# 32-row diagonal blocks inverted by substitution in a DeltaNet layer, in place of 16-row blocks and two merge products, and another order for the last two head groups

## The chip, the cores and the metric

The kernel runs on one core of a Trainium2 chip. The time is the device time in microseconds of one execution; the kernel before was run three times (median 3007.27 us). One further execution was taken with the hardware profiler; its span runs from the first to the last instruction. A core has the engines TensorE (PE, with its weight loads listed as PEld), VectorE (DVE), ScalarE (ACT), GpSimd (POOL) and SyncE (SP, which here issues the transfers).

## The reference: what is computed

A trunk of two layers works on 272 tokens (16 meta tokens and 256 others) of 2048 features in float32: a gated DeltaNet layer, then a differential-attention layer, each followed by a squared-ReLU MLP. The change lies in the DeltaNet layer alone. It has 32 value heads of 128 features on 16 query and key heads. What matters of it, cut:

```python
def step(S, xs):
    qc, kc, vc, bc, gc = xs
    G = jnp.cumsum(gc, axis=-1)
    decay = jnp.exp(jnp.where(tri_incl, G[..., :, None] - G[..., None, :], -jnp.inf))
    kb = kc * bc[..., None]
    a_kk = jnp.where(tri_strict, jnp.einsum('bhik,bhjk->bhij', kb, kc) * decay, 0.0)
    rhs = jnp.concatenate([vc * bc[..., None], kb * jnp.exp(G)[..., None]], axis=-1)
    sol = lax.linalg.triangular_solve(a_kk, rhs, left_side=True, lower=True, unit_diagonal=True)
    ...
```

For each head and each chunk of tokens a system with a unit lower triangular matrix is solved, and the state S is carried on from chunk to chunk.

## The kernel before, in words

**Order of the work.** The kernel goes through eight groups (line 1075) of four value heads each. A group has four stages of projections on TensorE: keys and queries (`keys`, line 653, four weight tiles), values (`values`, line 803, four), gates (`gates`, line 836, four) and the output product (`gate_out`, line 1048, four), the last one for the group two earlier (`LAG`). A weight tile is 1 MB; SyncE loads it (line 121), ScalarE and VectorE split it into a high and a low part (lines 138 and 140), and TensorE makes three products of each 128-row step of it (`mm3`, lines 153, 156 and 157). Such a step is called a k-step here; a weight tile has 16, a stage 64. There are three buffers for weight tiles and three each for the split halves.

**The planner.** Beside the projections runs the triangular part, written as generators. `Flow` (line 51) holds them with due times: each k-step advances its clock by 3 x 272 / 2400 = 0.34 us (line 158), and a generator's `yield t` puts its next piece t later. `until` (line 83) runs pieces early when the next stage needs them: a third value tile of a group waits until the core of the group before has finished two chunks (lines 809 and 828). This gives the order in which instructions are written; a scheduler then gives each engine its queue, in which an instruction can be pulled ahead while a more urgent one is not ready. Each engine then works its queue strictly in order.

**The triangular part of a group.** The tokens form chunks of 128, 128 and 16 (`CH`). `products` (line 683) makes the matrices `UA` for each chunk and head and writes their 16 x 16 diagonal blocks to memory (`scr`, line 762; the meta-sized last chunk's four blocks to `scr3`, line 744). `solve` (line 779) reads them back with one block a partition (`na`, 64 + 4 partitions), inverts them by substitution on VectorE (`forward`, line 641: 15 steps of a multiply and a reduction, on 16 columns at once, each multiply over 16 x (i + 1) elements), writes the result to memory (lines 793, 794) and loads it into the diagonal blocks of `DT` and `DT3` (lines 797, 801). It is written 40 us of the planner ahead of the core (`SOLVE`; 35 for the last group).

**The core** (line 846) first builds from the 16-row inverses those of 32-row blocks, `merge` (line 881), for chunks 0 and 1: it masks `UA` to the 32-row diagonal blocks, less the 16-row ones (line 884, GpSimd), transposes `DT` in blocks of 32 (line 890, VectorE), makes two products for each of four heads with a copy between them (lines 894, 896, 900), adds (line 902), transposes again (line 904), and makes a third product, `ps_n` (line 908), whose result `NT` serves to solve across the four 32-row blocks by a short series (`apply`, line 962; three products `ps_a`). Then come `ps_w`, the state `ps_s`, the output `ps_o`, and, for chunk 2, products with `DT3` (line 947). The turned outputs (`turned`, line 854, `ps_ot`) are multiplied with the gates, split (`halves`, line 1036) and go into `gate_out`. Small products are float32; the profile lists two records for each.

**The end.** For the last group `HOLD` puts the output product of two groups earlier ahead of the gates (lines 1082 to 1089), and the output products of the last two groups follow.

Of the kernel before, what the change touches and what calls it, by code (L numbers as in the profile page):

```python
# [10 lines left out]
F32 = mybir.dt.float32  # L11
# [3 lines left out]
ALU = mybir.AluOpType  # L15
AX = mybir.AxisListType

P = 128
D = 2048
KT = D // P  # L20
HD = D // 2
NM = 16
SEQ = 256
# [480 lines left out]
def gdn(ctx, tc, a, e):  # L504
    nc = tc.nc
    const, npool, dram, psm = (e[k] for k in ("const", "npool", "dram", "psm"))
# [6 lines left out]
    gc = ctx.enter_context(tc.tile_pool(name="gc", bufs=1))  # L513
# [16 lines left out]
    def work(name):  # L530
        return gt.tile([P, HB, P], F32, tag="g1", name=name, bufs=G1)
# [87 lines left out]
    nc.vector.memset(DT, 0.0)  # L619
    DT3 = gc.tile([TQ, TQ], F32, name="DT3")  # L620
    nc.vector.memset(DT3, 0.0)
    KQ3 = gc.tile([P, 2, 2 * TQ + TQ - NM], F32, name="KQ3")
    nc.vector.memset(KQ3, 0.0)

# [16 lines left out]
    def forward(na, xt):  # L641

        parts, w, n = xt.shape
        tmp = gt.tile([parts, w, n], F32, tag="fw_t", name="fw_t", bufs=1)
        for i in range(1, n):
            b = na[:, None, 0:i + 1, i].broadcast_to([parts, w, i + 1])
            nc.vector.tensor_tensor(tmp[:, :, 0:i + 1], xt[:, :, 0:i + 1], b, ALU.mult)
            nc.vector.tensor_reduce(xt[:, :, i], tmp[:, :, 0:i + 1], AX.X, ALU.add)

    def heads(t, b):  # L650
        return t[:, :, HB * b:HB * b + HB].rearrange("p c (h r) -> p c h r", r=2)
# [31 lines left out]
    def products(b, g, st):  # L683
# [4 lines left out]
        for t in range(2):  # L688
# [37 lines left out]
        scr = dram.tile([2, HB, 8, NM, NM], F32, name="scr")  # L726
        scr3 = dram.tile([HB, NM, NM], F32, name="scr3")
        UA = g["UA"] = []
        for c, (o, n) in enumerate(CH):
# [18 lines left out]
            for h in range(2):  # L748
# [11 lines left out]
            for bl in range(8):  # L760
                q = slice(NM * bl, NM * bl + NM)
                nc.sync.dma_start(scr[c, :, bl].rearrange("h j i -> j h i"), ua[q, :, 0, q])
            below(ua, NM)
# [9 lines left out]
    def below(ua, n):  # L773

        um = ua[:, :, 0, :].rearrange("p h (b i) -> p h b i", i=n)
        nc.gpsimd.affine_select(um, um, pattern=[[0, HB], [n, P // n], [0, n]], base=-1, channel_multiplier=-1,
                                compare_op=ALU.is_ge, fill=0.0)

    def solve(scr, scr3):

        nb = 2 * HB * 8
        na = gt.tile([nb + HB, NM, NM], F32, tag="na", name="na", bufs=1)
        xt = gt.tile([nb + HB, NM, NM], F32, tag="xt", name="xt", bufs=1)
        diag = lambda t: t.rearrange("p j i -> p (j i)")[:, 0:NM * NM:NM + 1]
        nc.gpsimd.memset(xt, 0.0)
        nc.gpsimd.memset(diag(xt), 1.0)
        nc.sync.dma_start(na[:nb], scr.rearrange("c h b j i -> (c h b) j i"))
        nc.sync.dma_start(na[nb:], scr3)
        nc.vector.memset(diag(na), 1.0)
        forward(na, xt)  # L790
        scr2 = dram.tile([nb, NM, NM], F32, name="scr2")
        scr4 = dram.tile([HB, NM, NM], F32, name="scr4")
        nc.sync.dma_start(scr2, xt[:nb])
        nc.sync.dma_start(scr4, xt[nb:])
        for bl in range(8):
            q = slice(NM * bl, NM * bl + NM)
            nc.sync.dma_start(DT[q, :, :, q].rearrange("p c h j -> p (c h) j"),
                              scr2.rearrange("(x b) m j -> b m x j", b=8)[bl])
        for h in range(HB):
            q = slice(NM * h, NM * h + NM)  # L800
            nc.sync.dma_start(DT3[q, q], scr4[h])

    def values(b, g):

# [31 lines left out]
    def gates(b, g):  # L836

        oT = g["oT"] = gk.tile([P, HB, L], F32, tag="oT", name="oT", bufs=LAG + 1)
        for hv in range(HB):
            ps = proj(64 + HB * b + hv)  # L840
            t = gt.tile([P, L], F32, tag="g272", name="zt", bufs=GB)
            nc.scalar.activation(t, ps[:, :L], AF.Tanh, scale=0.5)
            nc.vector.scalar_tensor_tensor(oT[:, hv], t, 1.0, ps[:, :L], ALU.add, ALU.mult)
            g["gates"] += 1

    def core(b, g):
# [31 lines left out]
        def flat(t):  # L878
            return t.rearrange("p h j -> p (h j)")

        def merge(c):

            us = work("us")
            nc.gpsimd.affine_select(us.rearrange("p h (b i) -> p h b i", i=32),
                                    UA[c][:, :, 0, :].rearrange("p h (b i) -> p h b i", i=32),
                                    pattern=[[0, HB], [-32, 4], [0, 32]], base=0, channel_multiplier=1,
                                    compare_op=ALU.is_ge, fill=0.0)
            below(UA[c], 32)
            e16 = work("e16")
            nc.vector.transpose(flat(e16), flat(DT[:, c]))  # L890
            yield step
            _, pE = bank("ps_e")
            for hv in range(HB):
                nc.tensor.matmul(pE[:, hv], us[:, hv], e16[:, hv], start=True, stop=True)
            ae = work("ae")
            nc.scalar.copy(ae, pE)
            yield step
            _, pD = bank("ps_d")
            for hv in range(HB):
                nc.tensor.matmul(pD[:, hv], ae[:, hv], DT[:, c, hv], start=True, stop=True)  # L900
            d32 = work("d32")
            nc.vector.tensor_tensor(d32, DT[:, c], pD, ALU.add)
            dn = work("dn")
            nc.vector.transpose(flat(dn), flat(d32))
            yield step
            _, pN = bank("ps_n")
            for hv in range(HB):
                nc.tensor.matmul(pN[:, hv], dn[:, hv], UA[c][:, hv, 0, :], start=True, stop=True)
            NT = work("NT")
            nc.scalar.copy(NT, pN)  # L910
            merged[c] = d32, NT
            yield step

        yield from merge(0)
# [427 lines left out]
```

## Time and profile before

| what | value |
|---|---|
| median of three runs | 3007.27 us (3007.19 to 3008.01) |
| the profiled execution's own time | 3007.38 us |
| its span, first to last instruction | 3004.7 us |
| mean granted TensorE clock | 0.994 |
| TensorE busy, weight loads busy | 99%, 97% of the span |
| VectorE, ScalarE, GpSimd busy | 64%, 49%, 7% |
| the DeltaNet groups | about the first 1023 us (last output-product addition, line 1064, at 1022.9) |
| moved by DMA | 488.32 MB, 163 GB/s in the mean |

How to read the profile. A group of instructions is told by line, engine, operation and what it writes from what it reads; busy time is the sum of durations, and idle time ahead of a group is put down to what ended it. Matmuls overlap, so the time that one takes from TensorE is read from start to start and not from durations. The granted clock is the share of full speed that TensorE was given in a stretch. Many instructions share the line of a helper (lines 138, 140, 153 to 157), so they are told apart by the tile that they write.

### The profile page before, as it was taken

The numbers are of one execution on the slowest core, as the hardware profiler recorded it, in microseconds if no ns is written. First come the engines' busy times: TensorE is split into PE (matmuls) and PEld (weight loads), VectorE is DVE, ScalarE is ACT, GpSimd is POOL, SyncE is SP. The second block draws the span as 40 slices with busy tenths as digits, with TensorE's granted clock in tenths as the row PEclk, the third lists the DMA queues.
The fourth block names the chain that finished last, engine by engine and source line by source line (L and its number), as shares of the span: only waits on it lengthen the run. The fifth ranks groups of instructions, "written<-read, shape, count | busy, mean of one in ns | idle before, by whom it ended". The sixth has DMA issues, their size and how long they took to land. (4 is left out here: it accounts for less than half of the span.)

```text
span 3004.7 us, 56783 instructions
## 1 busy us (share of the span) xinstructions
PE 2965.7 (99%) x23595; PEld 2920.7 (97%) x23595; DVE 1929.2 (64%) x3391; ACT 1465.2 (49%) x2616; POOL 214.3 (7%) x216
## 2 busy tenths in 40 slices
PE   8999999999999899999999999999999999999998
PEld 8999999999999899999999999999999999999998
DVE  7777576776767764555555568777647455555555
ACT  4556555465564554344434444455555444444443
POOL 0110011010100310000000004200013000000001
PEclk9999999999999899999999999999999999999999
DMA  5443443434433354545444444433354555555553
GB/s 205 160 139 123 156 152 135 158 124 155 153 128 143 130 196 171 181 169 178 173 172 180 170 172 151 151 131 142 138 205 163 190 187 183 185 188 189 183 183 112
DMA packets 94992, 488.32 MB, mean 163 GB/s; under 512 B 31632, under 2 KB 35056, under 8 KB 37264
## 3 DMA queue, kind: packets, MB, share of 16 engines
q1 hardware_dynamic: 94736, 484.71, 45.2%
q8 instruction: 185, 3.03, 0.4%
q14 instruction: 71, 0.58, 0.1%
HBM read 481.41 MB, written 3.25 MB: 161 GB/s over the span
## 5 line engine op out<-in xcount | busy, mean ns | idle before, releaser
L140 DVE TENSOR_TENSOR wlo<-wraw,whi 128x1024 fp32r<-128x1024 f32 x872 | 1072.3, 1232 | 766.2 <-ACT whi L138 763.9
L138 ACT ACTIVATE whi<-wraw 128x1024 fp32r<-128x1024 f32 x890 | 940.1, 1059 | 1125.1 <-PE ps_dn L157 435.8
L156 PE MATMUL ps_dn<-yh,wlo 128*128 128x272 f32 (+1 forms) x2048 | 585.8, 286 | 0.0
L156 PE MATMUL ps_up<-xh,wlo 128*128 128x272 f32 (+1 forms) x2048 | 583.7, 286 | 0.2 <-DVE wlo L140 0.2
L157 PE MATMUL ps_dn<-yl,whi 128*128 128x272 f32 (+1 forms) x2048 | 583.3, 285 | 0.0
L153 PE MATMUL ps_up<-xh,whi 128*128 128x272 f32 (+1 forms) x2048 | 581.4, 284 | 0.0
L153 PE MATMUL ps_dn<-yh,whi 128*128 128x272 f32 (+1 forms) x2048 | 581.3, 284 | 0.0
L157 PE MATMUL ps_up<-xl,whi 128*128 128x272 f32 (+1 forms) x2048 | 581.2, 285 | 0.1
L153 PE MATMUL ps_in<-xh,whi 128*128 128x272 f32 x1520 | 460.2, 303 | 0.0
L157 PE MATMUL ps_in<-xl,whi 128*128 128x272 f32 x1520 | 440.3, 290 | 0.8 <-DVE xl L321 0.8
L156 PE MATMUL ps_in<-xh,wlo 128*128 128x272 f32 x1520 | 438.8, 289 | 0.0
L153 PEld LDWEIGHTS ps_up<-xh,whi 128*128 128x128 f32 x2048 | 386.6, 189 | 0.6 <-ACT xh L402 0.2
L153 PEld LDWEIGHTS ps_dn<-yh,whi 128*128 128x128 f32 x2048 | 386.8, 189 | 0.0
L157 PEld LDWEIGHTS ps_dn<-yl,whi 128*128 128x128 f32 x2048 | 386.7, 189 | 0.0
L157 PEld LDWEIGHTS ps_up<-xl,whi 128*128 128x128 f32 x2048 | 385.7, 189 | 0.4 <-DVE xl L410 0.3
L156 PEld LDWEIGHTS ps_up<-xh,wlo 128*128 128x128 f32 x2048 | 383.9, 188 | 0.5 <-DVE wlo L140 0.5
L156 PEld LDWEIGHTS ps_dn<-yh,wlo 128*128 128x128 f32 x2048 | 384.3, 188 | 0.0
L153 PEld LDWEIGHTS ps_in<-xh,whi 128*128 128x128 f32 x1520 | 286.5, 189 | 4.2 <-issue 2.1
L156 PEld LDWEIGHTS ps_in<-xh,wlo 128*128 128x128 f32 x1520 | 286.8, 189 | 1.2 <-issue 0.2
L157 PEld LDWEIGHTS ps_in<-xl,whi 128*128 128x128 f32 x1520 | 285.8, 188 | 1.2 <-DVE xl L321 1.0
L476 DVE TENSOR_TENSOR acc<-acc,ps_dn 128x272 f32<-128x272 f32 (+1 forms) x224 | 96.1, 429 | 125.5 <-PE ps_dn L157 125.5
L153 PE MATMUL ps_at<-xh,whi 128*128 128x272 f32 x512 | 154.6, 302 | 0.0
(342 smaller groups left out, 4415.3 us busy)
## 6 DMA issues: line engine op xcount, KB each, us to landing
wraw<-w_up SPq DMA_DIRECT2D x128, 1024.0 KB
wraw<-w_down SPq DMA_DIRECT2D x128, 1024.0 KB
wraw<-w_in SPq DMA_DIRECT2D x97, 1024.0 KB
wraw<-w_out SPq DMA_DIRECT2D x32, 1024.0 KB
wraw<-w_kv SPq DMA_DIRECT2D x32, 1024.0 KB
wraw<-w_q SPq DMA_DIRECT2D x16, 1024.0 KB
wraw<-w_o SPq DMA_DIRECT2D x16, 1024.0 KB
gb<-g_dram SPq DMA_DIRECT2D x8, 544.0 KB
```

Source lines behind the costliest of these rows:

```text
L138: nc.scalar.activation(hi, part, AF.Copy)
L140: inst = eng.tensor_tensor(lo, part, hi.bitcast(F32), ALU.subtract)
L153: one = nc.tensor.matmul(ps, wh, rh, start=(k == 0), stop=False)
L156: nc.tensor.matmul(ps, wl, rh, start=False, stop=False)
L157: ring["mm"] = nc.tensor.matmul(ps, wh, rl, start=False, stop=(k == nk - 1))
L476: nc.vector.tensor_tensor(acc[:, m, :N], acc[:, m, :N], ps[:, :N], ALU.add)
```

## The change

- The blocks are 32 x 32 (`NS`), four a chunk (`NBL`). Eight transfers of blocks a group write to `scr` in place of sixteen. `na` holds each of the 32 blocks of a group in four copies, one for every fourth column, on 128 partitions; `xt` holds 8 columns of 32 rows a partition. `forward` makes 31 steps; at step i it works on the first i // 4 + 1 columns, up to 8. The unit entries of `xt` are copied by ScalarE from a small tile (`e4`), itself built once by a reduction. The four 16-row blocks of the last chunk get a substitution of their own, one column a partition on 64 partitions, 15 steps.
- `forward` and `solve` are generators now: a pause of 2 after every fourth step (`RUN`, `RUNGAP`), one of 16 after the loads are issued (`LANDS`). What waits after the solve is 22 in place of 40, and 18 in place of 35 in the last group.
- `merge` keeps only the transpose, `ps_n` and `NT`: the masked copy, the second mask, the first transpose, the products `ps_e` and `ps_d`, the copy `ae` and the addition go, with two pauses.
- The work buffers for the core are 7 in place of 9 (`G1`).
- The seventh group's gates come after the eighth group's keys and values, ahead of the sixth group's output product.

The diff, cut to its core:

```diff
-G1 = 9
+G1 = 7
-STEP7 = (2.0, 5.0, 35.0)
-SLACK, UGAP, SOLVE, STEP, OTURN = 6.0, 1.2, 40.0, 3.0, 14.0
+STEP7 = (2.0, 5.0, 18.0)
+SLACK, UGAP, SOLVE, STEP, OTURN = 6.0, 1.2, 22.0, 3.0, 14.0
...
+    def forward(na, xt, w, per, name):
+
+        parts, n = na.shape[0], na.shape[1]
+        tmp = gt.tile([parts, w, n], F32, tag=name, name=name, bufs=1)
         for i in range(1, n):
-            b = na[:, None, 0:i + 1, i].broadcast_to([parts, w, i + 1])
-            nc.vector.tensor_tensor(tmp[:, :, 0:i + 1], xt[:, :, 0:i + 1], b, ALU.mult)
-            nc.vector.tensor_reduce(xt[:, :, i], tmp[:, :, 0:i + 1], AX.X, ALU.add)
+            k = min(w, i // per + 1)
+            b = na[:, None, 0:i + 1, i].broadcast_to([parts, k, i + 1])
+            nc.vector.tensor_tensor(tmp[:, :k, 0:i + 1], xt[:, :k, 0:i + 1], b, ALU.mult)
+            nc.vector.tensor_reduce(xt[:, :k, i], tmp[:, :k, 0:i + 1], AX.X, ALU.add)
+            if i % RUN == RUN - 1:
+                yield RUNGAP
...
-        solve(scr, scr3)
+        yield from solve(scr, scr3)
...
         nc.gpsimd.memset(xt, 0.0)
-        nc.gpsimd.memset(diag(xt), 1.0)
-        nc.sync.dma_start(na[:nb], scr.rearrange("c h b j i -> (c h b) j i"))
-        nc.sync.dma_start(na[nb:], scr3)
-        nc.vector.memset(diag(na), 1.0)
-        forward(na, xt)
...
+        for r in range(4):
+            nc.scalar.copy(flat(xt)[:, r:r + (NS + 4) * (NS // 4 - 1) + 1:NS + 4], e4[:, r:r + 1].broadcast_to([P, NS // 4]))
+        nc.scalar.copy(xs[:, 0], eye_s)
+        blocks = scr.rearrange("c h b j i -> (c h b) (j i)")
+        nc.sync.dma_start(flat(na), blocks[None, :, :].broadcast_to([4, P // 4, NS * NS]))
+        nc.sync.dma_start(flat(ns), scr3.rearrange("h j i -> h (j i)")[:, None, :].broadcast_to([HB, NM, NM * NM]))
+        yield LANDS
+        nc.vector.memset(flat(na)[:, 0:NS * NS:NS + 1], 1.0)
+        nc.vector.memset(flat(ns)[:, 0:NM * NM:NM + 1], 1.0)
+        yield from forward(na, xt, NS // 4, 4, "fw_t")
+        scr2 = dram.tile([P // 4, NS, NS], F32, name="scr2")
+        for q, cols in enumerate(scr2.rearrange("x (s q) j -> q x s j", q=4)):
+            nc.sync.dma_start(cols, xt[P // 4 * q:P // 4 * (q + 1)])
+        yield from forward(ns, xs, 1, NM, "fw_s")
...
         def merge(c):
 
-            us = work("us")
-            nc.gpsimd.affine_select(us.rearrange("p h (b i) -> p h b i", i=32),
...
-            below(UA[c], 32)
-            e16 = work("e16")
-            nc.vector.transpose(flat(e16), flat(DT[:, c]))
-            yield step
-            _, pE = bank("ps_e")
-            for hv in range(HB):
-                nc.tensor.matmul(pE[:, hv], us[:, hv], e16[:, hv], start=True, stop=True)
-            ae = work("ae")
-            nc.scalar.copy(ae, pE)
-            yield step
-            _, pD = bank("ps_d")
-            for hv in range(HB):
-                nc.tensor.matmul(pD[:, hv], ae[:, hv], DT[:, c, hv], start=True, stop=True)
-            d32 = work("d32")
-            nc.vector.tensor_tensor(d32, DT[:, c], pD, ALU.add)
             dn = work("dn")
-            nc.vector.transpose(flat(dn), flat(d32))
+            nc.vector.transpose(flat(dn), flat(DT[:, c]))
             yield step
             _, pN = bank("ps_n")
...
         values(b, gs[b])
+
+        if b == NB - 1:
+            gates(b - 1, gs[b - 1])
         if b >= NB - HOLD and b >= LAG:
             gate_out(b - LAG, gs[b - LAG])
-        if b != 1:
+        if b not in (1, NB - 2):
             gates(b, gs[b])
```

More of the change, by code (lines that the diff above doesn't have):

```diff
@@ L22 @@
 NM = 16
+NS = 32
+NBL = P // NS
+RUN, RUNGAP, LANDS = 4, 2.0, 16.0
 SEQ = 256
@@ L621, in gdn @@
     nc.vector.memset(DT3, 0.0)
+    eye_s = gc.tile([HB * NM, NM], F32, name="eye_s")
+    e4 = gc.tile([P, 4], F32, name="e4")
+    nc.vector.tensor_reduce(e4, ident.rearrange("p (q x) -> p q x", q=4), AX.X, ALU.add)
+    nc.vector.tensor_reduce(eye_s, ident[:HB * NM, :HB * NM].rearrange("p (h j) -> p j h", j=NM), AX.X, ALU.add)
     KQ3 = gc.tile([P, 2, 2 * TQ + TQ - NM], F32, name="KQ3")
@@ L725, in products @@
                                 compare_op=ALU.is_ge, fill=NEG)
-        scr = dram.tile([2, HB, 8, NM, NM], F32, name="scr")
+        scr = dram.tile([2, HB, NBL, NS, NS], F32, name="scr")
         scr3 = dram.tile([HB, NM, NM], F32, name="scr3")
@@ L759, in products @@
                 yield UGAP
-            for bl in range(8):
-                q = slice(NM * bl, NM * bl + NM)
+            for bl in range(NBL):
+                q = slice(NS * bl, NS * bl + NS)
                 nc.sync.dma_start(scr[c, :, bl].rearrange("h j i -> j h i"), ua[q, :, 0, q])
-            below(ua, NM)
+            below(ua, NS)
         g["laid"] = True
@@ L790, in solve @@
-        forward(na, xt)
[L791 to L796, printed above, removed]
+        na = gt.tile([P, NS, NS], F32, tag="na", name="na", bufs=1)
+        ns = gt.tile([HB * NM, NM, NM], F32, tag="ns", name="ns", bufs=1)
+        xt = gt.tile([P, NS // 4, NS], F32, tag="xt", name="xt", bufs=1)
@@ new lines, in solve @@
+        xs = gt.tile([HB * NM, 1, NM], F32, tag="xs", name="xs", bufs=1)
+        flat = lambda t: t.rearrange("p j i -> p (j i)")
+        nc.gpsimd.memset(xt, 0.0)
+        for r in range(4):
[3 more added lines that the diff above has]
+        nc.sync.dma_start(flat(na), blocks[None, :, :].broadcast_to([4, P // 4, NS * NS]))
@@ L797, in solve @@
+        yield from forward(ns, xs, 1, NM, "fw_s")
+        scr4 = dram.tile([HB * NM, NM], F32, name="scr4")
+        nc.sync.dma_start(scr4, xs[:, 0])
+        for bl in range(NBL):
+            q = slice(NS * bl, NS * bl + NS)
             nc.sync.dma_start(DT[q, :, :, q].rearrange("p c h j -> p (c h) j"),
-                              scr2.rearrange("(x b) m j -> b m x j", b=8)[bl])
+                              scr2.rearrange("(x b) m j -> b m x j", b=NBL)[bl])
         for h in range(HB):
@@ L910, in merge @@
             nc.scalar.copy(NT, pN)
-            merged[c] = d32, NT
+            merged[c] = DT[:, c], NT
             yield step
```

12 lines of the change are left out of this document (1 added, 11 removed).

## Prediction

> **What bounds the kernel now.** I read the page's table of engines first, then the engines' busy time in stretches, then what TensorE waited for.
>
> ```profile
> PE 2965.7 (99%) x23595; PEld 2920.7 (97%) x23595; DVE 1929.2 (64%) x3391; ACT 1465.2 (49%) x2616; POOL 214.3 (7%) x216
> ```
> ```profile
> 500.00:600.00 100.00, 100.00 (x791) 98.39 (x790) 75.05 (x161) 51.30 (x106) 9.36 (x11) 1.00 0.45 155
> 600.00:700.00 100.00, 100.00 (x780) 97.82 (x779) 75.65 (x165) 55.69 (x132) 8.46 (x11) 1.00 0.42 147
> ```
> ```profile
> PE ps_ot L864 <- ACT ov L1030: 3.5, 1, 3.5
> PE ps_ot L861 <- ACT ov L1027: 3.2, 1, 3.2
> PE ps_e L894 <- DVE e L890: 0.7, 1, 0.7
> ```
>
> In the stretches the columns after the length are PE, PEld, DVE, ACT and POOL busy, the granted clock, the DMA share and GB/s. While the DeltaNet groups run, PE is busy 100 of 100 us, DVE 75, ACT 51 to 56. So a matmul that leaves gives its time back, unless DVE, which takes over the work, runs out of its 25% of air. The third fence holds three of TensorE's waits: the two at ps_ot belong to the end of the last group, when no other matmuls are left; the third is the first merge product, waiting for its transposed block.
>
> **The removed products.** TensorE's timeline around one product of each kind (start, duration, line, count):
>
> ```profile
> 573.84 0.29 PE L153 MATMUL ps_in<-xh,whi 128*128 128x272 f32 x1
> ...
> 574.58 1.05 PE L894 MATMUL ps_e<-e,us 128*128 128x128 f32 x8
> 575.39 0.37 PE L153 MATMUL ps_in<-xh,whi 128*128 128x272 f32 x1
> 575.60 0.29 PE L156 MATMUL ps_in<-xh,wlo 128*128 128x272 f32 x1
> ```
> ```profile
> 595.87 1.05 PE L894 MATMUL ps_e<-e,us 128*128 128x128 f32 x8
> 596.76 1.06 PE L965 MATMUL ps_a<-z,NT 128*128 128x128 f32 x8
> ```
> ```profile
> L894 PE MATMUL ps_e<-e,us x128: 270/275/348, 147.8 to 951.0; 128*128 128x128 f32 x128
> L900 PE MATMUL ps_d<-DT,ae x128: 271/275/377, 149.6 to 955.0; 128*128 128x128 f32 x128
> ```
>
> Durations overlap, so I go by starts. Six projection matmuls, two k-steps, start from 573.84 on, and the product at 574.58: 0.123 us each, 0.37 a k-step. The eight records of a product (four heads, two records each) hold the array from 574.58 to 575.39, and the projection matmul behind them lasts until 575.60. That matmul would alone have taken 0.12, so the product costs 1.02 less 0.12, 0.90 us. Between other products it costs 596.76 less 595.87, 0.89. There are 128 records each of ps_e and ps_d, 16 + 16 products, all in a stage where TensorE has no gap to hide them in: 16 x 0.90 + 16 x 0.89 = **28.6 us** removed. The 0.7 us wait for the first transposed block goes with its product.
>
> **What is added on VectorE.** The substitution grows from 15 steps on 16 columns to 31 steps on up to 8 columns, plus 15 small steps for the meta block.
>
> ```profile
> L647 DVE TENSOR_TENSOR fw_t<-xt,na 68x256 f32<-68x256 f32 x8 | 4.8, 606 | 0.2
> L647 DVE TENSOR_TENSOR fw_t<-xt,na 68x32 f32<-68x32 f32 x8 | 1.5, 187 | 0.6
> L648 DVE TENSOR_REDUCE xt<-fw_t 68x16 f32<-68x256 f32 x8 | 3.3, 411 | 0.0
> L648 DVE TENSOR_REDUCE xt<-fw_t 68x16 f32<-68x32 f32 x8 | 1.5, 181 | 0.2
> L890 DVE STREAM_TRANSPOSE e<-DT 128x512 f32<-128x512 f32 x16 | 11.3, 708 | 6.9 <-DMA DT<-scr 6.9
> L902 DVE TENSOR_TENSOR d<-DT,ps_d 128x512 f32<-128x512 f32 x16 | 10.9, 683 | 4.7 <-PE ps_d L900 4.6
> ```
>
> From 32 to 256 elements the multiply rises 419 ns over 224 elements, 1.87 ns each on 127 fixed; the reduction 1.03 ns on 148. Before, 2160 elements in 15 steps: (127 + 148) x 15 = 4.1 us, and 2.90 ns x 2160 = 6.3 us, together 10.4. After, the large one has 31 steps and 3047 elements (sum over i of min(8, i//4 + 1) times i + 1): 8.5 + 8.8 = 17.4 us; the small one 15 steps and 135 elements: 4.1 + 0.4 = 4.5. So 21.9 for 10.4, 11.5 more a group. Two transposes and two additions leave, 2 x 0.708 + 2 x 0.683 = 2.8. Net 8.7 us a group, 70 us over eight. The groups' rhythm stands in SyncE's transfers of the last two:
>
> ```profile
> 760.36 0.46 SPq L787 DMA_DIRECT2D na<-scr  x1
> ```
> ```profile
> 882.77 0.46 SPq L787 DMA_DIRECT2D na<-scr  x1
> 921.00 0.47 SPq L793 DMA_DIRECT2D scr<-xt  x1
> 927.22 1.76 SPq L801 DMA_DIRECT2D DT<-scr  x4
> ```
>
> A group takes 882.77 - 760.36 = 122.4 us, so 8.7 us more takes DVE from about 75% to about 82%. It all lies beside matmuls: cost on the path **0**, covered by DVE's idle time; if that were gone, every added microsecond would show. The two reductions that build the unit columns once at the start cost at most two of 0.41 us there, 0.
>
> The Trainium skill, "VectorE: DVE Perf Modes", section "Rules for kernel authors", speaks against this exchange: it tells authors to minimize the count of operations and calls tensor_reduce the slowest one. Here the count goes from 30 to 92 a group, which is a real charge (the fixed parts make 12.7 of the 21.9 us), but the trace does not bear out the order: at 256 elements the reduction takes 411 ns and the multiply 606. At the page's one element per cycle of 0.96 GHz for both, the large substitution would be an estimated 14.9 us, not 17.4; neither reaches the path.
>
> **What is moved or added elsewhere, with one answer each.** ScalarE loses two 128x512 copies a group and gains five of 128x8 or less; at 51 to 56% busy, no cost. GpSimd loses two copies with a mask and two masks; it is 7% busy. SyncE issues 27 small transfers a group for 36; the number of weight loads stays. The blocks now travel in four copies, 512 KB for 64 KB a group, which over 122 us is under 4 GB/s beside the 147 to 155 of the rows above: 0. Eighth group's keys and values ahead of seventh's gates: on SyncE eight weight loads pass four, on ScalarE and VectorE their splits do, on TensorE 128 k-steps pass 64; the same work in another order, 0 by itself. It puts the 64 k-steps of the gates between the eighth group's blocks and the point where they are needed. Fewer work buffers (7 for 9): four names that lived in them are gone (us, e16, ae, d32); 0.
>
> **A wait that is added.** The unit entries of xt move from GpSimd to ScalarE copies, which wait for GpSimd's memset, which waits for the transfer of the previous xt to land. ScalarE runs in order: behind a held copy stand the weight splits (whi), behind them wlo and the matmuls.
>
> ```profile
> POOL xt L785 <- DMA scr<-xt: 122.2, 5, 30.0
> SPq L797 <- DMA scr<-xt: 24.9, 8, 3.8
> SPq L793 <- DVE xt L648: 5.0, 3, 3.5
> SPq L121 <- DVE wlo L140: 1205.7, 194, 28.2
> ```
>
> GpSimd does stand waiting for that landing, which cost nothing since nobody was behind it. The same landing held SyncE 24.9 us in 8 times, 3.1 each. If ScalarE is held as long, the weights already split must cover it; they covered SyncE's holds, which TensorE's waits don't show. Bounds: 0 and 8 x 3.1 = 25 us; a gain is excluded, since the copies do nothing that anyone got earlier. I take **+2 us**, near the lower end, because a hold of about 3 us has shown no loss in this trace; the 25 stay in the range.
>
> **The end of the last group.** TensorE's end of the eighth group:
>
> ```profile
> 941.15 1.05 PE L908 MATMUL ps_n<-UA,dn 128*128 128x128 f32 x8
> 985.20 0.43 PE L947 MATMUL ps_w<-R,DT 64*64 64x128 f32 x2 [0.83 <-ACT ov L944]
> 989.11 0.48 PE L864 MATMUL ps_ot<-ident,ov 128*128 128x128 f32 x1 [3.48 <-ACT ov L1030]
> 994.34 0.36 PE L861 MATMUL ps_ot<-ident,ov 64*128 64x64 f32 x1 [3.20 <-ACT ov L1027]
> 995.53 0.60 PE L153 MATMUL ps_out<-oh,whi 128*128 128x272 f32 x1 [0.82 <-ACT oh L1043]
> ```
> ```profile
> 990.00:995.00 5.00, 1.50 (x6) 0.69 (x5) 2.92 (x14) 0.87 (x3) 0.00 (x0) 0.50 0.00 0
> 995.00:1000.00 5.00, 4.47 (x19) 4.47 (x20) 1.96 (x6) 1.80 (x5) 0.00 (x0) 0.50 0.01 3
> ```
>
> From ps_n to the last output product the chain takes 995.53 - 941.15 = 54.4 us, and from 985.20 on TensorE has nothing else: 3.48 + 3.20 + 0.82 + 0.83 = 8.3 us of waits, then matmuls at clock 0.50. Counting the planner's due times (each k-step of three projection matmuls advances it 0.34 us; each yield as written), the eighth group's first ps_n falls 68 k-steps ahead of the last gate_out before, and 75 after. Seven steps of 0.37 us are **2.6 us** by which the bubble shrinks, if the blocks have arrived. Have they? Before, 927.22 + 1.76 - 882.77 = 46.2 us from na to the last transfer, with 10.4 us of substitution stretched over about 32; 17.4 us stretched alike are 51, so some 65 us. The planner gives 177 k-steps from solve to ps_n for 121 before, 56 x 0.37 = 21 us more than the 941.15 - 882.77 = 58.4 it had: 79.5. It fits by 14 us, less what the start slips: by the planner's due times the seventh group's core is now emitted in one rush ahead of the eighth's third value tile, and the eighth's second block matrix waits for a buffer of that core's first chunk. The slip isn't in this trace; its bounds are 0 and one chunk of the chain above, 54.4 / 2 = 27 us. I take it under 14, since a chunk ends some stages before its half.
>
> **The sum.** The profiled execution took 3007.38 us for a span of 3004.7; the median of the runs is 3007.27, so the two stand for each other. 3007.4 - 28.6 - 0.7 - 2.6 + 2 = **2977.5 us**, 1.0% faster.
>
> **Rivals.** *The last blocks come late.* The slip uses up the 14 us and 6 more; TensorE idles longer at the end and runs longer at clock 0.50. Price 6, the 2.6 not gained and 2.5 of half clock over another 5 us: 2977.5 + 11.1 = 2988.6. For it: the stretch factor of 3 in the last group, and the rush. Against it: the substitution would now lie beside gates, which give DVE less to do for each weight tile than the output products with their four additions.
>
> *Slower: SyncE is held by the substitution's end.* The transfers out of xt wait in SyncE's queue for the last reduction, and the weight loads stand behind them. Until now that hold was 3.5 us at most (third row above), and SyncE usually waits for free weight buffers, 194 times, so it runs ahead. One weight tile feeds 48 matmuls, 5.9 us. From a hold of about 7 us on (a tile in hand and one being split) TensorE starves for the rest. If the longer substitution ends 12 us later than planned in each group, that is 8 x 5 = 40 us: 3018. Against it: by the planner the first ps_n of a middle group is due 191 k-steps after its solve for 144 before, 47 x 0.37 = 17 us more for 7.0 us more work in the large substitution.
>
> *TensorE's time isn't freed.* If another engine paced these stages, nothing is gained, 3007. Against it stands PE 100 of 100 with DVE at 75.
>
> *The bubble closes enough to keep the clock.* If the waits at ps_ot shrink by some 3 us, the matmuls from 995.53 on no longer run at half clock: another 2.5 us in 995 to 1000 and the shrunk waits, 2972. The Trainium skill, "TensorE: Matmul & The Clock Gate", section "HAM oscillation", has the rule that an idle gap above some 3.4 us throttles the array; the row with 3.48 us followed by clock 0.50 agrees.
>
> **How the numbers follow.** Forecast 0.63, late blocks 0.17, SyncE held 0.07, no freed time 0.06, clock kept 0.07. A measurement of this kernel can tell about 0.2%, 6 us. Faster: 0.63 + 0.17 + 0.07 = 0.87; same 0.06; slower 0.07. The range goes from 2967 (the clock kept and all 8.3 us of waits gone, not 3) to 2997 (late blocks with a third of the 25 us of ScalarE holds). It leaves out SyncE held and no freed time, 0.13, and little of the rest.
>
> **What would show it.** No ps_e and ps_d; TensorE at 100 of 100 in the middle groups with a period near 118.8 us (122.4 less 4 x 0.9); DVE there near 82%; the large multiply at 256 elements near 0.6 us and 92 substitution operations a group; the waits at the two ps_ot again one each and a little smaller. Wrong would be: new TensorE waits in the middle groups, on wlo or whi; SyncE waiting over 7 us for the last reduction; ps_n of the eighth group waiting for its transposed block.

## The result, and the profile after

The changed kernel takes 3037.35 us in the median of four runs (3036.33 to 3037.59), the kernel before in the same comparison 3007.23 (3005.93 to 3008.01). The ratio is 1.0099, 95% interval 1.0087 to 1.0111: slower by 30 us, where 30 us less was forecast. The profiled execution has a span of 3035.2 us at a mean granted clock of 0.988 (before 3004.7 and 0.994). Times below are medians of a kernel's executions; one execution, of the kernel before without its merge products, took 5776.74 us where the three others took 2972.39 to 2972.61, and is left out.

The table of engines of the changed kernel, and its busy time in stretches of 100 us (PE, PEld, DVE, ACT and POOL, then granted clock, DMA share, GB/s):

```profile
PE 2956.3 (97%) x23339; PEld 2905.8 (96%) x23339; DVE 1968.8 (65%) x3865; ACT 1459.4 (48%) x2640; POOL 169.5 (6%) x176
```
```profile
100.00:200.00 100.00, 88.88 (x670) 86.33 (x668) 66.13 (x180) 45.82 (x103) 4.41 (x7) 0.95 0.50 149
200.00:300.00 100.00, 91.96 (x669) 87.42 (x669) 78.52 (x245) 57.15 (x159) 5.59 (x9) 0.95 0.35 120
500.00:600.00 100.00, 96.80 (x746) 93.54 (x745) 78.44 (x220) 51.94 (x122) 3.30 (x6) 1.00 0.43 143
600.00:700.00 100.00, 97.21 (x751) 93.96 (x750) 75.76 (x213) 56.53 (x137) 2.99 (x5) 1.00 0.41 140
700.00:800.00 100.00, 91.61 (x700) 89.47 (x699) 64.67 (x133) 50.77 (x121) 3.32 (x6) 0.97 0.45 143
```

The 256 matmul records of `ps_e` and `ps_d` are gone (23339 for 23595). But in six of the eight stretches from 100 to 900 us PE no longer fills its time: 89 to 97 of 100 us where it had been 99 to 100. The other engines don't fill it either. In the first and the last of these rows DVE, too, is only at 66.13 and 64.67 (73.64 and 72.25 before). Engines that idle together suggest a wait for something that isn't an engine.

What VectorE waited for while the DeltaNet groups ran (us in total, times, longest), in the changed kernel and then in the kernel before:

```profile
DVE wlo L143 <- ACT whi L141: 116.0, 122, 3.7
DVE na L805 <- DMA na<-scr: 43.0, 8, 9.9
```
```profile
DVE na L789 <- DMA na<-scr: 0.8, 2, 0.5
```

The second line is new in size. The instruction at line 805 is the 0.09 us memset that writes ones on the diagonal of `na`, the first of VectorE that touches the tile. It waits in each of the eight groups for the tile to land, 43.0 us in all, for 0.8 before. VectorE works its queue in order, so everything behind the memset waits too. What TensorE waited for in the same stretch:

```profile
PE ps_ks L938 <- DVE S L998: 11.8, 2, 8.0
PE ps_a L964 <- DVE z L975: 8.7, 1, 8.7
PE ps_v L835 <- DVE vt L647: 6.4, 3, 2.9
PE ps_in L159 <- DVE wlo L143: 4.5, 1, 4.5
```

Four different tiles, all written by VectorE: the state, the series of the solve, a value tile, the low weight half. None of these instructions is itself slow. They stand behind the memset. The second group shows it in full, on SyncE, on VectorE and on TensorE (start, duration, line, then in brackets the idle time before and what ended it):

```profile
189.14 0.57 SPq L802 DMA_DIRECT2D na<-scr  x1
```
```profile
191.41 1.23 DVE L143 TENSOR_TENSOR wlo<-wraw,whi 128x1024 fp32r<-128x1024 f32 x1 [1.31 <-ACT whi L141]
192.55 0.43 DVE L647 SCALAR_TENSOR_TENSOR vt<-ps_in,cv_a 128x272 f32<-128x272 f32 x1
202.47 0.09 DVE L805 MEMSET na<- 128x32 f32 x1 [9.49 <-DMA na<-scr]
202.66 0.16 DVE L656 TENSOR_TENSOR fw_t<-xt,na 128x2 f32<-128x2 f32 x1
202.86 0.15 DVE L657 TENSOR_REDUCE xt<-fw_t 128x1 f32<-128x2 f32 x1
202.93 0.68 DVE L975 TENSOR_TENSOR z<-R,ps_a 128x512 f32<-128x512 f32 x1
203.53 1.22 DVE L143 TENSOR_TENSOR wlo<-wraw,whi 128x1024 fp32r<-128x1024 f32 x1
```
```profile
193.04 1.05 PE L964 MATMUL ps_a<-t,NT 128*128 128x128 f32 x8
...
194.65 0.29 PE L159 MATMUL ps_in<-xh,wlo 128*128 128x272 f32 x1
203.66 2.08 PE L964 MATMUL ps_a<-z,NT 128*128 128x128 f32 x8 [8.73 <-DVE z L975]
```

SyncE issues the transfer at 189.14; the memset that waits for its landing starts 13.3 us later. VectorE reaches the memset at 192.98, 3.8 us after the issue where the planner had put 16 (`LANDS`), and stands for 9.49 us. The result of the `ps_a` of 193.04 waits for its addition (`z`, 202.93), and TensorE's next matmul in order is a `ps_a` that reads that `z`, so the projections behind it don't run either. From 194.65 to 203.66 no matmul starts. The product that ends the gap takes 2.08 us instead of 1.05.

### The profile page after: what moved, and what is told of

Read it like the earlier page. It is cut to its first block, busy times and chain, and to the rows that moved or that the text cites. A ratio compares the mean times of both kernels' runs of the same rounds, so it can differ in the third digit from the quotient of the medians.

```text
span 3035.2 us, 56614 instructions
## 1 busy us (share of the span) xinstructions
PE 2956.3 (97%) x23339; PEld 2905.8 (96%) x23339; DVE 1968.8 (65%) x3865; ACT 1459.4 (48%) x2640; POOL 169.5 (6%) x176
## 5 line engine op out<-in xcount | busy, mean ns | idle before, releaser
L160 PE MATMUL ps_in<-xl,whi 128*128 128x272 f32 x1520 | 446.4, 294 | 0.8 <-DVE xl L324 0.8
L156 PE MATMUL ps_out<-oh,whi 128*128 128x272 f32 x512 | 153.3, 299 | 3.4 <-DVE acc L1063 2.5
```

What stands on the lines that cost most here:

```text
L156: one = nc.tensor.matmul(ps, wh, rh, start=(k == 0), stop=False)
L160: ring["mm"] = nc.tensor.matmul(ps, wh, rl, start=False, stop=(k == nk - 1))
```

## The experiments

Two theories stood against each other from the trace. A: the transfer of `na` is slow and VectorE's in-order wait for it makes the loss. B: the longer substitution is simply too much for VectorE. C came with them, from the prediction's own worry: the new order of the last groups writes the core in one rush. Each kernel is compared with the kernel before on the same chip.

**Four transfers in place of one.**

```
-        nc.sync.dma_start(flat(na), blocks[None, :, :].broadcast_to([4, P // 4, NS * NS]))
+        for q in range(4):
+            nc.sync.dma_start(flat(na)[P // 4 * q:P // 4 * (q + 1)], blocks)
```

> The changed kernel with one edit: the block copies reach na by four transfers of 32 partitions each, in place of one whose outermost step is four. Theory A (VectorE is held: its memset of na's diagonal stands in its queue waiting for a transfer that takes 7 to 11 us, and TensorE runs dry behind it): the landing takes 5 to 7 us from its issue, VectorE's 43 us of waits for na fall under 12, TensorE's long gaps in the middle groups go, time 2980 to 2995. Theory B (VectorE has too much work with the longer substitution): nothing changes by more than 6 us, 3031 to 3043. Theory C (the core written in one rush ahead of the third value tile): the same as B.

Measured: 2985.98 us (2983.72 to 2988.68), ratio 0.9929, interval 0.9914 to 0.9944. So 51.4 us less than the changed kernel, with the same bytes, the same substitution and the same order of groups. Its transfers (KB each, median us from issue to landing), its table of engines and two of its stretches:

```profile
na<-scr SPq DMA_DIRECT2D x32, 128.0 KB, 2.6
```
```profile
PE 2942.5 (99%) x23339; PEld 2894.5 (97%) x23339; DVE 1965.0 (66%) x3865; ACT 1460.0 (49%) x2640; POOL 171.7 (6%) x176
```
```profile
600.00:700.00 100.00, 99.88 (x771) 96.93 (x770) 80.29 (x224) 53.17 (x120) 3.30 (x6) 1.00 0.45 154
700.00:800.00 100.00, 100.00 (x779) 97.60 (x779) 81.08 (x229) 59.07 (x144) 3.79 (x5) 1.00 0.44 150
```

VectorE has no wait for `na` left, PE is back at 100 in these stretches, and DVE at 80 to 81 is about where the prediction put it. The transfers land sooner than the 5 to 7 us expected. Of the 51.3 us between the two spans (3035.2 and 2983.9) TensorE spends 37.5 idle (78.9 us for 41.4), and the other 13.8 are longer busy time for the same 23339 matmuls (2956.3 for 2942.5): the mean granted clock is 0.988 in the one and 0.995 in the other.

**Two transfers, the other way.**

```
-        nc.sync.dma_start(flat(na), blocks[None, :, :].broadcast_to([4, P // 4, NS * NS]))
+        for q in range(2):
+            nc.sync.dma_start(flat(na)[P // 2 * q:P // 2 * (q + 1)],
+                              blocks[None, :, :].broadcast_to([2, P // 4, NS * NS]))
```

> The changed kernel with one edit that makes the suspected transfer slower: two transfers of 64 partitions, each with an outermost step of two. Theory A: the same bytes over half as many DMA engines take about 16 to 20 us to land, VectorE is held some 10 us longer in each of eight groups, time 3090 to 3130. Theory B and theory C: within 10 us of the changed kernel, 3030 to 3047.

Measured: 3061.91 us (3060.13 to 3063.86), ratio 1.0180, interval 1.0163 to 1.0197. Two transfers are slower than one; their outermost step is 2 (the packets are counted further down). The size is below what was expected, the direction is as theory A says, and B and C have no reason for any change. VectorE's wait:

```profile
DVE na L806 <- DMA na<-scr: 68.1, 8, 11.3
```

**The reductions left out** (the kernel then doesn't compute the inverses). In `forward`:

```
-            nc.vector.tensor_reduce(xt[:, :k, i], tmp[:, :k, 0:i + 1], AX.X, ALU.add)
```

> The changed kernel with the 46 reductions a group of the substitution left out (its results are then not the inverses): VectorE loses about 10 us of work a group and comes back to the load of the kernel before, while the transfer of the blocks stays as it is. Theory A: the waits for na stay near 43 us and the time at 3020 to 3040. Theory B: the stalls go, 2975 to 2990. Theory C: 3025 to 3040.

Measured: 3035.99 us (3029.07 to 3044.53), ratio 1.0096, interval 1.0076 to 1.0117: not to be told from the changed kernel, although some 80 us of VectorE's work are gone. The waits for `na` are still there, 38.7 us in the profiled execution, the shortest of the four. B falls as the main cause.

**The merge products left out of the kernel before.**

```
-            us = work("us")
...
-            for hv in range(HB):
-                nc.tensor.matmul(pE[:, hv], us[:, hv], e16[:, hv], start=True, stop=True)
...
-            nc.vector.transpose(flat(dn), flat(d32))
+            nc.vector.transpose(flat(dn), flat(DT[:, c]))
```

> The kernel before with its merge step left out but for the transpose, ps_n and NT (the blocks then stay 16 rows, and the result is not the inverse): the worth of the removed products by themselves. By the prediction's term, 28.6 us of TensorE and 0.7 of waiting: 2975 to 2982. If the products filled time that TensorE would have lost anyway: above 3000.

Measured: 2972.61 us in three executions, against 3007.06 before, ratio 0.9884, interval 0.9868 to 0.9901. In the kernel before, the products with their copies, masks and additions are worth 34.5 us, a little more than expected. So there is a gain to be had; how much of it the changed kernel keeps in its middle groups is read below.

**The same slow transfer, a longer planned delay.**

```
-RUN, RUNGAP, LANDS = 4, 2.0, 16.0
+RUN, RUNGAP, LANDS = 4, 2.0, 28.0
```

> The changed kernel with the one broadcast transfer kept as slow as it is, and only the planner's delay between it and VectorE's first instruction on its tile raised from 16 to 28 of its microseconds. Theory A (VectorE stands in order behind a tile that lands late): the waits of VectorE for na fall from 43.0 us in 8 to under 5 us, the long gaps of TensorE between 112 and 925 us go, and the time falls to 2983 to 3000 us, near the kernel with four transfers (2986), although the transfer itself still takes 7 to 11 us. Rival D (the transfer on four of the sixteen DMA engines disturbs other things, a transfer of weights behind it on the same engines for instance): nothing is won by waiting later, 3030 to 3040. Rival E (a later substitution is late for the last group's core): the gaps in the middle go, but those at the last group grow by up to 12 us, 2995 to 3005.

Measured: 3060.53 us (3059.86 to 3063.14), ratio 1.0175, interval 1.0158 to 1.0192. All expectations missed. VectorE's and TensorE's waits:

```profile
DVE na L805 <- DMA na<-scr: 65.6, 8, 9.6
```
```profile
PE ps_ks L938 <- DVE S L998: 37.3, 7, 6.8
```

The waits rose, so this kernel didn't do what its edit was meant to do. The planner's delay sets where an instruction is written; the scheduler then orders each engine's queue anew and pulls a piece ahead when it takes it to be ready. Counted by the weight pieces (`wlo`) that stand before it in VectorE's queue, the memset of the eight groups comes behind 25, 48, 68, 96, 128, 160, 192 and 218; in the changed kernel behind 25, 46, 65, 96, 128, 160, 192 and 217. It hardly moved, but the state updates (line 998), which in the fourth group of the changed kernel stand ahead of the memset, now stand behind it, as VectorE's timeline of this kernel shows:

```profile
411.96 0.69 DVE L978 TENSOR_TENSOR z<-z,ps_a 128x512 f32<-128x512 f32 x1 [1.25 <-PE ps_a L964]
422.27 0.09 DVE L805 MEMSET na<- 128x32 f32 x1 [9.62 <-DMA na<-scr]
...
423.88 1.11 DVE L998 SCALAR_TENSOR_TENSOR S<-S,eGL,ps_s 128x128 f32<-128x128 f32 x4
```

**The same slow transfer, the memset tied behind later weight pieces.** Here the place is forced by an ordering edge without a wait of its own:

```
+    flow.low = []
...
+                if urgent:
+                    flow.low.append(inst)
...
-        nc.vector.memset(flat(na)[:, 0:NS * NS:NS + 1], 1.0)
-        nc.vector.memset(flat(ns)[:, 0:NM * NM:NM + 1], 1.0)
+        for t, n in ((na, NS), (ns, NM)):
+            ones = nc.vector.memset(flat(t)[:, 0:n * n:n + 1], 1.0)
+            tc.add_manual_dep(ones.ins, flow.low[-4].ins.name, NOSYNC, reason="order")
```

> The changed kernel, its one transfer of the blocks unchanged. Only VectorE's two memsets on na and ns are tied to come behind the last but three of the weight pieces (wlo) that the planner has written by then, so in VectorE's order they stand two to three pieces later in six groups; in the first two groups that piece is already ahead of them and they stay where they are. Theory A (VectorE's in-order wait makes the loss, about 1.15 us of time for each us of it over the kernels run so far): the waits of the first two groups stay, some 17 us, the other six fall from 25 to under 8 us together, and the time is 3037 - 1.15 x 20 = 3014 us, within 3008 to 3022. Rival D (the slow transfer itself disturbs other work): the waits go and the time stays within 3030 to 3045. Rival E (a later substitution makes the last group's core late): the waits go but TensorE's gaps at the last group grow by 5 us or more, 3020 to 3030.

Measured: 3006.45 us (3002.61 to 3008.54), ratio 0.9996, interval 0.9987 to 1.0005. The places are now 25, 46, 67, 99, 131, 163, 195 and 219. VectorE's waits, and four stretches:

```profile
DVE na L809 <- DMA na<-scr: 16.7, 2, 9.1
```
```profile
100.00:200.00 100.00, 89.58 (x674) 87.03 (x672) 66.50 (x181) 46.38 (x105) 5.21 (x7) 0.96 0.52 150
200.00:300.00 100.00, 96.19 (x707) 91.69 (x708) 79.65 (x240) 60.02 (x167) 5.84 (x9) 0.95 0.38 127
...
500.00:600.00 100.00, 99.99 (x773) 97.09 (x772) 80.64 (x223) 53.43 (x120) 3.31 (x6) 1.00 0.46 154
600.00:700.00 100.00, 99.99 (x773) 96.99 (x772) 80.54 (x221) 54.53 (x130) 3.00 (x5) 1.00 0.44 147
```

This is the cleanest of the runs. In the two groups whose memset didn't move, the waits and TensorE's gaps stay (100 to 300 us); in the six where it moved by two or three pieces, VectorE has no wait for `na` and PE is at 99.8 to 100 of 100 from 300 to 890 us, with the transfer as slow as ever (its packets take 6.8 to 9.8 us in these groups). That refutes D, that the slow transfer itself disturbs other work: no loss shows where nobody stands in order behind it. The gain, 30.9 us for 26.3 us of waits, is a little beyond what theory A gave. Of E, the core that comes too late, nothing shows: TensorE's waits at the last group are 2.6, 3.2 and 0.8 us, as with four transfers.

**The order of the last groups, alone and undone.** The edit in the main loop, first undone in the changed kernel, then made alone in the kernel before, then undone with the four transfers:

```
-        if b == NB - 1:
-            gates(b - 1, gs[b - 1])
...
-        if b not in (1, NB - 2):
+        if b != 1:
```

> The changed kernel with the seventh group's gates back ahead of the eighth group's keys and values. Theory A: the loss sits in the eight waits for na, which stay, so the time stays within 3030 to 3045 us, with 35 to 50 us of VectorE's waits for na. Rival C (the new order makes the loss, with values and core written in a rush): 2980 to 3010 us.

> The kernel before, its 64-row blocks and merge products kept, with only the eighth group's keys and values put ahead of the seventh group's gates. Theory A gives the order next to nothing: 3003 to 3010 us. Rival C: slower by 10 us or more, 3017 to 3040.

> The changed kernel with the four transfers of 32 partitions and with the old order of the gates. With the waits for na gone, what is left of the order shows: if the new order feeds TensorE during the eighth group's substitution, this kernel is 2 to 8 us slower than the four transfers with the new order (2988 to 2994 against 2986); if the order is worth nothing, 2983 to 2989.

Measured: undone in the changed kernel 3058.04 us (ratio 1.0165, interval 1.0150 to 1.0180) with 56.7 us of waits for `na`; made alone in the kernel before 2999.70 (0.9974, 0.9963 to 0.9985), against 3007.84; undone with the four transfers 2995.15 (0.9959, 0.9944 to 0.9974), against 2985.98 with it. Rival C falls. The ranges that theory A gave for the first two were missed too: the first is slower than 3045 us, with more than 50 us of waits, and the second faster than 3003. The new order is worth 8.1 us in the kernel before and 9.2 us with four transfers, a little more than expected. In the changed kernel undoing it costs 20.7 us, and the waits for `na` grow by 13.7 with it.

**The last group's core sooner.** With four transfers TensorE still waited 6.6 us at the end of the last group (2.56, 3.20 and 0.83 us in its profile; the 7.5 us of the expectation is too much). On top of the four transfers:

```
-STEP7 = (2.0, 5.0, 18.0)
+STEP7 = (2.0, 5.0, 8.0)
```

and, in the second kernel, 4.0.

> Four transfers of 32 partitions as in the first experiment (2986.0 us), and the last group's core written 8 instead of 18 of the planner's microseconds behind its substitution. With four transfers TensorE still stood 7.5 us between the last group's core and the last projections (2.8, 3.5 and 1.2 us at 963 to 972 us). If that is because the core's last steps are written with no other matmuls among them, most of it goes: 2977 to 2982 us. If it is because the substitution ends too late for the core, the core waits for DT or the transposed block instead, and the time is 2984 to 2992 us.

> As the run before this one, with 4 instead of 8 of the planner's microseconds. If the substitution's end is not yet the limit, the same time as with 8 within 2 us, 2976 to 2982. If it becomes the limit here, the first matmuls of the last group's core (ps_n, ps_a) wait for the transposed block by some 3 to 5 us and it is that much slower than with 8.

Measured: 2987.18 us (ratio 0.9930, interval 0.9918 to 0.9942) and 2981.52 us (2979.63 to 2982.92; ratio 0.9911, interval 0.9896 to 0.9926). With 8 nothing is won: waits of 3.5 us at `ps_ot` and 0.8 us at `ps_out` stay. With 4 the core ends while output products are still there to fill in, and waits of 0.4 and 1.6 us are left between there and the layer's end. Neither of the two expectations for 4 foresaw that it would be 5.7 us faster than 8. The last group's first product, `ps_n`, has no wait even then, so the substitution isn't late. This version beats both kernels, before by 25.7 us.

**The reductions left out again, without the wait.** The edit of the third experiment, on the kernel just named:

> The kernel with four transfers and the core written 4 of the planner's microseconds behind the substitution (2981.5 us), with the 46 reductions a group left out (so the inverse isn't computed; 10.1 us of VectorE a group, 81 in all, go). If VectorE's added work lies beside matmuls once nothing waits for na, as the prediction priced it, the time stays within 2978 to 2985 us. Rival: at 79 to 84% busy VectorE already costs TensorE about 1 us a group through its weight pieces; then most of that goes with the reductions, 2968 to 2976.

Measured: 2976.99 us (2976.18 to 2978.76), ratio 0.9901, interval 0.9884 to 0.9917. The gain of 4.5 us puts it between the two expectations: the runs of the two kernels don't overlap, though the intervals of their ratios do. Two stretches of it:

```profile
500.00:600.00 100.00, 100.00 (x788) 98.47 (x787) 73.53 (x156) 51.80 (x114) 2.32 (x5) 1.00 0.46 157
600.00:700.00 100.00, 100.00 (x776) 97.32 (x775) 73.62 (x178) 53.84 (x120) 3.31 (x6) 1.00 0.47 155
```

**The kernels with the new order and the core in its old place, by VectorE's wait for `na`.** The waits are those of the profiled execution, so its own time stands beside them.

| kernel | wait for `na`, us | profiled execution, us | above four transfers, per us of wait |
|---|---|---|---|
| four transfers | 0 | 2985.67 | |
| memset tied later | 16.7 | 3005.55 | 1.19 |
| reductions left out | 38.7 | 3029.07 | 1.12 |
| changed kernel | 43.0 | 3037.19 | 1.20 |
| longer planned delay | 65.6 | 3063.14 | 1.18 |
| two transfers | 68.1 | 3062.77 | 1.13 |

The time rises with the waits, by 1.1 to 1.2 us for each; the last two kernels can't be told apart. Part of what is lost beyond the wait itself is the clock at which TensorE comes back: in the first two stretches of the changed kernel the granted clock is 0.95.

## Why the prediction was wrong, point by point

**The step that failed** is "The blocks now travel in four copies, 512 KB for 64 KB a group, which over 122 us is under 4 GB/s ...: 0". It priced the bytes as a mean rate. What counted here is the time from issue to landing of one transfer, and who stands in order behind it. The part "A wait that is added" looked for new waits on ScalarE alone. VectorE's memset of `na` was not looked at, although its wait of 0.8 us stood in the profile of before, and no rival has this transfer landing late. It cost 51.4 us (changed kernel less four transfers).

Why did it take longer? The packet records of the trace give the 128 packets of 4 KB that fill `na`: 3.5 to 4.0 of them run at a time in the changed kernel, 1.9 to 2.0 in the kernel with two transfers, 7.7 to 13.8 with four transfers of 32 partitions. From the first packet's start to the last one's end it takes 6.8 to 11.0 us, 13.8 to 15.7 and 2.2 to 3.6. In a stretch of the changed kernel in which little else is moved, the DMA share shows the same (column before the last):

```profile
286.00:292.00 6.00, 5.71 (x41) 4.91 (x39) 2.46 (x5) 2.87 (x9) 0.00 (x0) 1.00 0.25 85
```

The share is a quarter of the sixteen DMA engines. The pattern's outermost step is 4 in the changed kernel, 2 in the second experiment and 32 partitions in the first. The Trainium skill, "DMA: Bandwidth & Descriptors", section "Why a DMA increments its semaphore by 16 and not by 1", has the rule for it: a transfer is spread over the largest number of engines, at most 16, that divides the outermost sizes above 1 of both its patterns, here 4, 2 and 16. The traces agree for 4 and 2, with 3.5 to 4.0 and 1.9 to 2.0 packets at a time; up to 13.8 at a time fits 16 without showing it.

**The removed products, 28.6 + 0.7 us.** Right in direction. Left out of the kernel before they bring 34.5 us (by the interval 29.8 to 39.7); transposes, additions and steps of the last chain leave with them, which may be the rest; no trace of that kernel at this speed shows it. In the middle groups of the changed design they bring less than forecast. There the output-product stages start at 427.4, 549.8 and 672.1 us before, 122.3 apart, and at 416.5, 536.4 and 656.4 with four transfers, 119.9 to 120.0 apart with PE at 100, where 118.8 was forecast: 2.4 us a group for 3.6 (2.8 with the reductions left out, from starts at 416.6, 536.2 and 655.8). From start to start the two kinds of products had held TensorE for 3.4 us a group, and the matmuls that stay take some 0.9 us a group longer without them. Why they do is open.

**VectorE, 21.9 us a group at no cost.** The work was sized well. By groups, the changed kernel has:

```profile
L656 DVE TENSOR_TENSOR fw_t<-xt,na 128x2 f32<-128x2 f32 (+30 forms) x248 | 85.6, 345 | 2.4
L657 DVE TENSOR_REDUCE xt<-fw_t 128x1 f32<-128x2 f32 (+30 forms) x248 | 63.1, 255 | 2.3
L656 DVE TENSOR_TENSOR fw_s<-xs,ns 64x2 f32<-64x2 f32 (+14 forms) x120 | 18.9, 157 | 0.0
L657 DVE TENSOR_REDUCE xs<-fw_s 64x1 f32<-64x2 f32 (+14 forms) x120 | 17.4, 145 | 0.0
```
```profile
L656 DVE TENSOR_TENSOR fw_t<-xt,na 128x256 f32<-128x256 f32 x8 | 5.2, 651 | 0.1
L657 DVE TENSOR_REDUCE xt<-fw_t 128x8 f32<-128x256 f32 x8 | 3.4, 424 | 0.1
```

That is 185.0 / 8 = 23.1 us a group for 21.9, 92 operations, and 651 ns for the large multiply where 0.6 us was forecast. "Cost on the path **0**" is nearly right: with the wait gone, 80.5 us of reductions less (63.1 + 17.4) bring 4.5 us, 0.06 us for each. For the 70 us that the change adds, that is an estimated 4 us.

**The wait added on ScalarE, +2 us, bounds 0 and 25.** The wait is there and small. The copies of the unit entries waited for GpSimd's memset, in the changed kernel 4.0 us in all; what that cost TensorE wasn't measured:

```profile
ACT xt L799 <- POOL xt L797: 4.0, 3, 2.6
```

**The end of the last group, -2.6 us.** The bubble shrank by less. The same rows in the changed kernel:

```profile
1013.25 0.43 PE L946 MATMUL ps_w<-R,DT 64*64 64x128 f32 x2
1016.23 0.42 PE L883 MATMUL ps_ot<-ident,ov 128*128 128x128 f32 x1 [2.56 <-ACT ov L1029]
...
1021.41 0.37 PE L880 MATMUL ps_ot<-ident,ov 64*128 64x64 f32 x1 [3.20 <-ACT ov L1026]
```
```profile
1016.00:1021.00 5.00, 1.98 (x6) 1.14 (x6) 2.66 (x13) 1.57 (x7) 0.00 (x0) 0.53 0.00 0
1021.00:1026.00 5.00, 3.76 (x16) 3.58 (x17) 1.78 (x5) 1.74 (x5) 0.00 (x0) 0.50 0.00 0
```

The waits are 2.56, 3.20 and 0.83 us (the last in front of the first output product behind these rows, at 1022.60), 6.6 for 8.3 before: 1.7 us less where 2.6 was forecast, and the matmuls behind them run at half clock as before. Seven k-steps were counted from due times; the experiments with the core sooner show that what stands beside the last products doesn't follow the due times step by step (18 to 8 brought nothing, 4 brought 4.5 us). "The same work in another order, 0 by itself" was wrong too: alone, the order brings 8.1 us in the kernel before. The blocks were in time, as the prediction had it: the last group's `ps_n` has no wait.

**The rivals.** SyncE was indeed held at the transfers out of `xt` ("over 7 us" was a sign named), in the changed kernel by up to 8.2 us:

```profile
SPq L810 <- DVE xt L657: 29.7, 7, 8.2
```

With four transfers the longest is 6.7 us, and TensorE then has no wait for a weight piece in these groups, so no cost of these holds shows; what 8.2 us alone would cost wasn't tried. That TensorE's time isn't freed is refuted by the middle groups with four transfers, 2.4 us shorter with PE at 100. The clock wasn't kept at the end. Nor is a wait below the 3.4 us that this rival cites safe for it: in the changed kernel TensorE waited 2.94 us before 425.51, and the granted clock is 0.50 from 425.8 to 429.2. The sign "new TensorE waits ... on wlo" came once, 4.5 us, behind the memset and not behind SyncE.

**The sum.** The miss is 3037.4 - 2977.5 = 59.9 us, and 51.4 of it are the waits for `na`. The other 8.5 (2986.0 with four transfers for 2977.5) are small misses of both signs, which no run adds up. VectorE's work costs some 4 us (the estimate above) for 0. The middle groups gain 2.4 us each for 3.6, and part of those 4 is in that. The end of the last group gains 1.7 us for 2.6. Against these, the order gains 8 to 9 us for 0. And one part had no term: from the start of the last output-product matmul to the end, behind the DeltaNet layer, the profiled execution takes 1986.7 us with one transfer and with four, 1982.6 before. Put together, the runs without the products and with the new order would allow 3007.4 - 34.5 - 8.1 = 2964.8 us, and the best kernel with reductions left out takes 2977.0. Of the 12 us between, it takes 3.9 us behind the layer (1986.5); the rest is open.

## What to carry to other kernels

Price a transfer by the time until it lands and not by its bytes over a period, and look up for each tile that it fills which instruction touches it first: on an engine that works in order, a 0.09 us memset that waits holds the whole queue and, through it, TensorE. Keep the outermost step of a transfer's pattern large enough for all DMA engines (four transfers of 32 partitions beat one of 4 x 32 by 51 us here), or place the first reader behind work that doesn't need it. When a planned delay is to do this, read the place in the engine's queue afterwards: raising the delay from 16 to 28 moved the memset by at most three weight pieces and lost 23 us.

## What the runs showed of the hardware

The same 512 KB filled 128 partitions in 2.2 to 3.6 us as four transfers of 32 partitions, in 6.8 to 11.0 as one of 4 x 32, in 13.8 to 15.7 as two of 2 x 32. More transfers were faster or slower by their outermost step, not by their number.

TensorE's granted clock fell during the 9.0 us gap of the second group, in the changed kernel's stretch

```profile
196.00:202.00 6.00, 0.00 (x0) 0.00 (x0) 0.00 (x0) 0.00 (x0) 0.00 (x0) 0.59 0.65 117
```

in which no engine ran at all and the granted clock is 0.59 in the mean; the eight `ps_a` records behind it took 2.08 us for 1.05. In the traces' clock records the stretches at 0.50 within a run last 3.4, 6.8, 10.2 or 13.7 us. The length of a wait alone doesn't decide: one of 2.00 us at 878 us, in the kernel with the core at 4, was followed by 3.4 us at half clock, one of 1.99 us at the same place with four transfers by none.
